# Three of four weight sums of a seven-product MLP move to GpSimd, and the order of its products is derived anew

## The chip, the cores and the metric

The kernel runs on one core of a Trainium2 chip. The metric is the device time of one execution in microseconds (us). TensorE is called PE in the profile, VectorE DVE, ScalarE ACT, GpSimd POOL and SyncE SP; SP issues most of the loads.

## The reference

A decoder trunk of two layers over 256 tokens of width 2048: an attention mixer (MLA), then a Mamba-2 mixer, each followed by a dense MLP of width 8192. The change touches the two MLPs alone:

```python
def squared_relu_mlp(h, w_in, w_out):
    u = jax.nn.relu(h @ w_in)
    return (u * u) @ w_out
```

All values are float32. `h` is 256 x 2048, `w_in` 2048 x 8192, `w_out` 8192 x 2048; every weight is read from memory once per layer, in tiles of 128 x 1024 float32 (512 KB).

## The kernel before

**Split weights.** A float32 product is made of three fp32r products: a weight tile `raw` is split into `wh` (ScalarE, a copy to fp32r, line 102) and `wl = raw - wh` (VectorE, line 103), and the left operand is split in the same way. Every unit of work is one weight tile of 128 x 1024, so each unit costs ACT one copy and DVE one subtraction of 128 x 1024, whatever it is used for. The pools hold six `raw` tiles, four `wh` and four `wl`: the conversion of a unit can begin only when the unit four places ahead of it has been multiplied.

**The MLP.** The hidden width is worked off in eight steps p = 0 to 7. Step 0's hidden block is computed in the plain way ("c" units, eight for each of two column halves of 512, twelve matmuls each). In steps 1 to 7 the block of 256 x 2048 by 2048 x 1024 is computed with seven half-size products in place of eight (Winograd's form of Strassen's scheme): M1, N7, N5, N6, N4, M2, N3, each in four units d = 0 to 3 of six matmuls ("s" units). With b11, b12, b21, b22 the four quarters of the weights for one d, the right operands are

- M1: b11; M2: b21; N3: b22
- N7: b12 + b22; N5: b12 + b11; N6: b11 + (b12 + b22); N4: b21 + (N6's operand)

so four sums of 128 x 1024 per d, sixteen per step. The left operands (sums of `h`) are made once per MLP (`combinations`). The output product of the step before ("o" units, four for each of four column blocks, twelve matmuls each) fills in between: the hidden block of step p - 1 is multiplied by `w_out` while step p's is made.

**Who makes the sums before.** `seven` (lines 171 to 212): N7, N5 and N6 are DVE additions (line 183), made at conversion time, in place. N4 is made by a DMA: once N6's operand has been split, GpSimd's queue issues a load of b21 that adds onto the tile of b11 (line 199). The tile of b11 lies in a pool of its own, `rx` (four buffers), b12 and b22 in `raw`.

**Order.** TensorE's order is written out by `plan` and `merged` (lines 1333 to 1388): they walk a list of the seven products and a list of filler units ("c" and "o"), with estimates of TensorE's and VectorE's work. The same plan makes the list of weight loads (`sequence`). On the other engines the instructions of a step stand in an order found at build time. `Flow.next` keeps, ahead of the unit that TensorE is at, six units loaded and three converted (`ahead = (6, 3)`). After the last unit of a product, its bank in PSUM is combined with others on DVE (`after`, lines 598 and 599), goes through relu and square on ACT, and is transposed by TensorE (four matmuls, line 310), with the result split once more (DVE line 300). After the fourth unit of an output block DVE adds two PSUM banks of 128 x 512 to the residual (line 419).

Of the kernel before, what the change touches and what calls it, by code (L numbers as in the profile page):

```python
# [20 lines left out]
F32 = mybir.dt.float32  # L21
# [7 lines left out]
P = 128  # L29
# [29 lines left out]
class Unit:  # L59

    def __init__(self, key, nk, n, loads, make):
        self.key, self.nk, self.n, self.loads, self.make = key, nk, n, loads, make


class Load:
# [4 lines left out]
class Flow:  # L72


    def __init__(self, nc, pools, seq, ahead):
        self.nc, self.pools, self.ahead = nc, pools, ahead
        self.units = [u for entry in seq for u in entry(self)]
        self.loaded, self.done, self.at = 0, 0, 0
        self.split = {}

    def fetch(self, ld, cuts=None, beside=None):
# [24 lines left out]
    def narrow_halves(self, raw):  # L106
# [8 lines left out]
            out.append(t)  # L115
        return out

    def convert(self, upto):
        while self.done < min(upto, len(self.units)):
            self.load(self.done + 1)  # L120
            self.split[self.done] = self.units[self.done].make()
            self.done += 1

    def next(self, key):
        j, u = self.at, self.units[self.at]
        assert u.key == key, (u.key, key)
        self.load(j + 1 + self.ahead[0])
        self.convert(j + 1 + self.ahead[1])
        self.at += 1
        return u, self.split.pop(j)  # L130
# [39 lines left out]
def seven(layer, p, src):  # L170

    state = {}

    def quarter(d, i, j):
        return src[2 * i + d // 2, 2 * p + j][:, (d % 2) * 1024:(d % 2) * 1024 + 1024]

    def unit(flow, name, d):  # L180
        nc = flow.nc
        st = state.setdefault(d, {})
        add = lambda out, a, b: nc.vector.tensor_tensor(st[out].tile, st[a].tile, st[b].tile, ALU.add)
        halves = lambda q: flow.halves(st[q].tile, 1024)

        def make():
            if name == "N7":
                add("b22", "b12", "b22")
                out = halves("b22")
                if d in LATE5:  # L190
                    nc.gpsimd.dma_start(st["b12"].tile, quarter(d, 0, 0), accum_op=ALU.add)
                return out
            if name == "N5" and d not in LATE5:
                add("b12", "b11", "b12")
                return halves("b12")
            if name == "N6":
                add("b11", "b11", "b22")
                out = halves("b11")
                nc.gpsimd.dma_start(st["b11"].tile, quarter(d, 1, 0), accum_op=ALU.add)  # L199
                return out  # L200
            return halves({"M1": "b11", "N4": "b11", "N5": "b12"}.get(name, name))

        def load(k, pool, q):
            st[k] = Load(pool, quarter(d, *q))
            return st[k]

        loads = {"M1": lambda: [load("b11", "rx", (0, 0))],
                 "N7": lambda: [load("b12", B12, (0, 1)), load("b22", "raw", (1, 1))],
                 "M2": lambda: [load("M2", "raw", (1, 0))], "N3": lambda: [load("N3", "raw", (1, 1))]}
        return Unit(("s", layer, p, name, d), 2, 512, loads.get(name, list)(), make)  # L210

    return unit


class Trunk:
# [274 lines left out]
    def mlp(self, layer, gain):  # L490
        with ExitStack() as ctx:
            mp = ctx.enter_context(self.tc.tile_pool(name="mlp", bufs=1, reuse_waits="tile"))
            for name, n in (("rx", 4), ("ry", 1)):
                self.flow.pools[name] = ctx.enter_context(self.tc.tile_pool(name=name, bufs=n, reuse_waits="tile"))
            self.flow.ahead = (4, 3)
            self.mlp_body(mp, layer, gain)

    def combinations(self, mp, xa):


        nc = self.nc
        f, S = {}, {}

        def whole(i, t):
            pool = "rx" if len(f) < 3 else "ry"
            f[i, t] = self.flow.pools[pool].tile([P, 1024], F32, tag=pool, name=self.name("xf"))
            h, lo = (v.rearrange("p k n -> p (k n)").bitcast(F32) for v in xa[i, t])
            nc.vector.tensor_tensor(f[i, t], h, lo, ALU.add)
            return f[i, t]

        def put(name, src, pool):
            S[name] = [(self.ktile(self.xtp).rearrange("p a b -> p (a b)") if pool is None else
                        pool.tile([P, 1024], F32R, name=self.name("s" + name))).rearrange("p (k n) -> p k n", n=P)
                       for _ in range(2)]
            self.split_out(*[v.rearrange("p k n -> p (k n)") for v in S[name]], src)

        def less(out, a, b):
            nc.vector.tensor_tensor(out, a, b, ALU.subtract)
            return out

        def one():
            a21, a11 = whole(0, 1), whole(0, 0)
            a22 = whole(1, 1)
            less(a22, a21, a22)
            put("N5", a22, mp)
            f["s1"] = a22

        def two():
            put("N7", less(f[0, 1], f[0, 1], f[0, 0]), mp)
            put("N6", less(f[0, 0], f[0, 0], f["s1"]), mp)  # L530
            a12 = whole(1, 0)
            less(a12, a12, f[0, 0])

        def three():
            put("N3", f[1, 0], None)

        return S, (one, two, three)

    def mlp_body(self, mp, layer, gain):
# [65 lines left out]
        def after(name, p):  # L605
            if name == "M1":
                v["m1"] = self.scratch()
                nc.scalar.activation(v["m1"], bank["M1"], AF.Copy)
            elif name in ("N5", "N6"):
                v[name] = p  # L610
                if v.get("N5") != p or v.get("N6") != p:
                    return
                w, c, e = (self.scratch() for _ in range(3))
                sub(w, bank["N6"], v["m1"])
                plus(c, bank["N5"], w)
                plus(w, bank["N7"], w)
                plus(e, bank["N7"], c)
                v["w"], v["c"] = w, c
                turn(relu_in_place(e, 1), p, 1, 1, TR[0])
            elif name == "N4":  # L620
                sub(v["w"], bank["N4"], v["w"])
                turn(relu_in_place(v["w"], 1), p, 0, 1, TR[1])
            elif name == "M2":
                plus(v["m1"], bank["M2"], v["m1"])
                turn(relu_in_place(v["m1"], 0), p, 0, 0, TR[2])
            elif name == "N3":
                plus(v["c"], bank["N3"], v["c"])
                turn(relu_in_place(v["c"], 0), p, 1, 0, TR[3])
# [693 lines left out]
             "x7", "z5", "z6", "o2a", "z7", "o2b", "o3"]  # L1322


B12 = "raw"
WARM = 9
LATE5 = ()
TR = (10, 8, 7, 7, 5)
TR_GAP = 4
PAUSE = 2.7  # L1330


def merged(p, blocks):


    main = [(n, d) for d in range(4) for n in ("M1", "N7", "N5", "N6") if n != "N5" or d not in LATE5]
    late = [(n, d) for d in range(4) for n in ("N5", "N4") if n == "N4" or d in LATE5]
    second = [(n, d) for d in range(4) for n in ("M2",)] + [("N3", d) for d in range(4)]
    units = [(b, o) for b, n in blocks for o in range(n)]
    vector = {"M1": 1.22, "N4": 1.22, "M2": 1.22, "N3": 1.22}  # L1340
    pe = 28 * 1.36 + 2.72 * len(units) + 16 * 0.11
    ve = (40 - len(LATE5)) * 1.22 + 1.22 * len(units) + 1.37 * len(blocks) + 11 * 0.68
    t = work = 0.0
    rest, done, out = -9.0, {}, []

    def ready(n, d):
        if n in ("N4", "N5"):
            return t >= done.get(("N6", d), 1e9) + 12 or (n, d) in main
        if n == "M2":
            return t >= done.get(("M1", 3), 1e9) + 7  # L1350
        if n == "N3":
            return t >= max(done.get((q, 3), 1e9) for q in ("N5", "N6")) + 7
        return True

    while main or late or second or units:
        op = next((q for q in (late, main, second) if q and ready(*q[0])), None)
        filler = t >= rest and len(units) > (4 if p == 7 and op else 0)
        if filler and (op is None or work > t * ve / pe - 2):
            b, o = units.pop(0)
            out.append(b + (o,))  # L1360
            t, work = t + 2.72, work + 1.22
            if not units or units[0][0] != b:
                rest, work = t + (PAUSE if b[0] == "o" else 10), work + 1.37
        else:
            if op is None:
                op = late or second
            n, d = op.pop(0)
            out.append(("s", p, n, d))
            t, work = t + 1.36, work + (1.22 if n == "N5" and d in LATE5 else vector.get(n, 2.44))
            done[n, d] = t  # L1370
            if n in ("N5", "N6") and d == 3 and {("N5", 3), ("N6", 3)} <= set(done):
                work += 2.73
            elif d == 3 and n in ("N4", "M2", "N3"):
                work += 0.68
    return out


# [146 lines left out]
```

## Time and profile before

| what | value |
|---|---|
| median of three runs | 2311.22 us (2311.05 to 2311.95) |
| profiled execution, its own time | 2310.92 us |
| its span, first to last instruction | 2308.7 us |
| first MLP, seven-product steps | 301.5 to 893 us of the span |
| second MLP, last seven-product unit | at about 2248 us of the span |
| loads for the MLP through SP | 256 of `mi` and 256 of `mo` into `raw`, 56 of `mi` into `rx` |
| adding loads through POOL | 56 of `mi` onto `rx` |

The profile is of one execution. A line of a group gives the source line, engine, operation, output and inputs, shape, count, then busy time, mean duration in ns, and the idle time in front. A line of waits gives who waited for whom: us in total, times, longest. A line of the timeline gives start, duration, engine, line and operation; "x2" means two of them run into one another. Durations of one DVE or PE instruction overlap with the next one's by a little, so that the distance of two starts, where the engine never idles, is what an instruction costs. In the view of one line the three numbers are shortest, median and longest duration in ns.

### The profile page before, as it was taken

Reading aid. Unit: us, or ns where it says so; the run is one execution under the profiler, and the core shown is the slowest. Engines: PE = TensorE matmul, PEld = TensorE weight load, DVE = VectorE, ACT = ScalarE, POOL = GpSimd, SP = SyncE. Lnnn points to the kernel's source line nnn. Section 1 sums busy time; section 2 is a strip of 40 time slices with the busy share of each in tenths; the row PEclk is TensorE's granted clock in tenths of the full one; section 3 lists DMA queues with packets and bytes.
Section 4 is the critical chain, followed back from the end, with each engine's and each line's share of the span. In section 5 each row is a group of like instructions: output and inputs, shape, how many; then the busy total and the mean of one; then the engine's idle time right before and its main releaser. Section 6 shows DMA issues by size and latency. Waiting matters only on the chain.

```text
span 2308.7 us, 30782 instructions
## 1 busy us (share of the span) xinstructions
PE 2302.4 (100%) x11057; PEld 1912.2 (83%) x11057; DVE 1874.8 (81%) x2318; ACT 1421.2 (62%) x1995; POOL 187.1 (8%) x227
## 2 busy tenths in 40 slices
PE   9999999999999999999999999999999999999999
PEld 8888888888888888888888888888888888888887
DVE  7776697899899897677787667656989889989895
ACT  7775465566666656565676565545566656666663
POOL 1430000000000000000122001110000000000000
PEclk9999999999999999999999999999999999999999
DMA  8444677877887877665566656656687788788874
GB/s 317 147 132 150 204 234 242 263 238 251 263 243 249 269 208 247 195 210 177 173 204 200 218 188 203 190 187 201 203 251 235 255 263 248 242 267 240 249 232 162
DMA packets 152153, 510.77 MB, mean 221 GB/s; under 512 B 17152, under 2 KB 26304, under 8 KB 152000
## 3 DMA queue, kind: packets, MB, share of 16 engines
q1 hardware_dynamic: 143712, 479.37, 63.2%
q0 software_dynamic: 8064, 29.36, 7.7%
q8 instruction: 87, 1.43, 0.3%
q14 instruction: 66, 0.54, 0.1%
q10 hardware_dynamic: 224, 0.07, 0.0%
HBM read 506.58 MB, written 2.16 MB: 220 GB/s over the span
## 4 chain that ended last, share of the span: by engine, by line
PE 96%; DVE 2%; DMA 1%; issue 0%; ACT 0%; SPq 0%; DVEq 0%
PE acc L325 13%; PE acc L326 13%; PE acc L329 13%; PE yp L595 9%; PE yp L596 9%; PE yp L594 9%; PE st L595 7%; PE st L596 7%; PE st L594 7%; PE sm L310 2%; DMA wraw<-mi 1%; DVE wl L103 1%; PE y L1240 1%; PE acc L594 1%; PE acc L596 1%; PE acc L595 1%
## 5 line engine op out<-in xcount | busy, mean ns | idle before, releaser
L102 ACT ACTIVATE wh<-wraw 128x1024 fp32r<-128x1024 f32 (+1 forms) x818 | 861.2, 1055 | 640.1 <-PE acc L326 313.5
L103 DVE TENSOR_TENSOR wl<-wraw,wh 128x1024 fp32r<-128x1024 f32 (+1 forms) x818 | 985.1, 1217 | 271.3 <-ACT wh L102 257.3
L594 PE MATMUL yp<-wh,k 128*128 128x512 f32 x896 | 349.9, 391 | 0.0
L595 PE MATMUL yp<-wl,k 128*128 128x512 f32 x896 | 349.0, 389 | 0.5 <-DVE wl L103 0.5
L596 PE MATMUL yp<-wh,k 128*128 128x512 f32 x896 | 348.8, 389 | 0.0
L325 PE MATMUL acc<-wh,xt 128*128 128x512 f32 x704 | 281.4, 400 | 0.2 <-ACT wh L102 0.2
L326 PE MATMUL acc<-wh,xt 128*128 128x512 f32 x704 | 275.1, 391 | 0.0
L102 ACT ACTIVATE wh<-wrx 128x1024 fp32r<-128x1024 f32 x168 | 178.1, 1060 | 135.7 <-PE yp L596 105.5
L103 DVE TENSOR_TENSOR wl<-wrx,wh 128x1024 fp32r<-128x1024 f32 x168 | 204.1, 1220 | 36.1 <-ACT wh L102 35.9
L595 PEld LDWEIGHTS yp<-wl,k 128*128 128x128 f32 x896 | 168.3, 188 | 35.9 <-DVE wl L103 1.4
L596 PEld LDWEIGHTS yp<-wh,k 128*128 128x128 f32 x896 | 168.2, 188 | 35.0
L325 PE MATMUL acc<-wh,k 128*128 128x512 f32 x496 | 197.0, 397 | 0.0
L594 PEld LDWEIGHTS yp<-wh,k 128*128 128x128 f32 x896 | 168.2, 188 | 34.7
L326 PE MATMUL acc<-wh,k 128*128 128x512 f32 x496 | 193.3, 390 | 0.0
L329 PE MATMUL acc<-wl,xt 128*128 128x512 f32 x704 | 188.5, 389 | 0.0
L594 PE MATMUL st<-wh,xt 128*128 128x512 f32 x448 | 176.9, 395 | 0.0
L595 PE MATMUL st<-wl,xt 128*128 128x512 f32 x448 | 174.8, 390 | 0.0
L596 PE MATMUL st<-wh,xt 128*128 128x512 f32 x448 | 174.7, 390 | 0.0
L325 PEld LDWEIGHTS acc<-wh,xt 128*128 128x128 f32 x704 | 132.6, 188 | 28.4 <-ACT wh L102 1.5
L329 PEld LDWEIGHTS acc<-wl,xt 128*128 128x128 f32 x704 | 132.2, 188 | 28.0
L326 PEld LDWEIGHTS acc<-wh,xt 128*128 128x128 f32 x704 | 132.7, 189 | 27.2 <-issue 1.0
L199 POOL DMA_DIRECT2D wrx<-mi x56 | 48.8, 871 | 1140.8 <-DVE wl L103 1035.0
(302 smaller groups left out, 3450.4 us busy)
## 6 DMA issues: line engine op xcount, KB each, us to landing
wraw<-mi SPq DMA_DIRECT2D x256, 512.0 KB, 5.1
wraw<-mo SPq DMA_DIRECT2D x256, 512.0 KB, 5.2
wraw<-si SPq DMA_DIRECT2D x160, 512.0 KB, 4.4
wraw<-so SPq DMA_DIRECT2D x64, 512.0 KB, 4.5
wrx<-mi SPq DMA_DIRECT2D x56, 512.0 KB, 5.1
wrx<-mi POOLq DMA_DIRECT2D x56, 512.0 KB, 8.2
wraw<-wo SPq DMA_DIRECT2D x32, 512.0 KB, 3.8
wraw<-ukv SPq DMA_DIRECT2D x16, 512.0 KB, 4.1
```

The lines of the kernel that those rows point to most:

```text
L102: self.last = nc.scalar.activation(h[:, v], raw[:, v], AF.Copy)
L103: nc.vector.tensor_tensor(lo[:, v], raw[:, v], h[:, v].bitcast(F32), ALU.subtract)
L199: nc.gpsimd.dma_start(st["b11"].tile, quarter(d, 1, 0), accum_op=ALU.add)
L310: self.nc.tensor.transpose(b[:, j * P:(j + 1) * P], src[:, j * P:(j + 1) * P], self.ident)
L325: nc.tensor.matmul(accs[t][:, :n], ah, wh[:, q, :], start=first and kt + q == 0, stop=False)
L326: nc.tensor.matmul(accs[t][:, :n], al, wh[:, q, :], start=False, stop=False)
L329: nc.tensor.matmul(accs[t][:, :n], lhs(kt + q, t)[0], wl[:, q, :], start=False, stop=en and q == nk - 1)
L594: nc.tensor.matmul(b, ah, wh, start=first and q == 0, stop=False)
L595: nc.tensor.matmul(b, ah, wl, start=False, stop=False)
L596: nc.tensor.matmul(b, al, wh, start=False, stop=last and q == 1)
L1240: nc.tensor.matmul(y[t][c, o], part(t)[:, c], xg[g][t][:, o], start=True, stop=True)
```

## The change

For each d the step now has four loads: b11, b12, b22 and b21 (M1, N7, N4), and later b21 and b22 once more for M2 and N3, as before. N7's sum stays with VectorE; N5, N6 and N4 are summed by GpSimd's `tensor_tensor` (twelve per step, 168 in all); no DMA adds any longer, and b21 for N4 is a plain load through SP into `raw`. b11 and b12 lie in a pool `sum` with five buffers. Sums have a counter of their own in `Flow`: they are issued two units ahead of the conversion (`SUM_AHEAD = 2`), so five ahead of TensorE. N5 and N6 no longer share an "either may come last" rule: N6 is the later one.

```diff
+    def sums(self, upto):
+        while self.added < min(upto, len(self.units)):
+            self.load(self.added + 1)
+            if self.units[self.added].add:
+                self.units[self.added].add()
+            self.added += 1
...
         self.load(j + 1 + self.ahead[0])
+        self.sums(j + 1 + self.ahead[1] + SUM_AHEAD)
         self.convert(j + 1 + self.ahead[1])
...
-            if name == "N5" and d not in LATE5:
-                add("b12", "b11", "b12")
-                return halves("b12")
-            if name == "N6":
-                add("b11", "b11", "b22")
-                out = halves("b11")
-                nc.gpsimd.dma_start(st["b11"].tile, quarter(d, 1, 0), accum_op=ALU.add)
-                return out
...
+        def add(out, a, b):
+            eng = flow.nc.vector if name in VSUM else flow.nc.gpsimd
+            return lambda: eng.tensor_tensor(st[out].tile, st[a].tile, st[b].tile, ALU.add)
...
+            "N7": (lambda: [load("b12", 0, 1), load("b22", 1, 1)], "b22", add("b22", "b12", "b22")),
+            "M1": (lambda: [load("b11", 0, 0)], "b11", None),
+            "N5": (list, "b12", add("b12", "b11", "b12")),
+            "N6": (list, "b11", add("b11", "b11", "b22")),
+            "N4": (lambda: [load("b21", 1, 0)], "b21", add("b21", "b11", "b21")),
+            "M2": (lambda: [load("M2", 1, 0)], "M2", None),
+            "N3": (lambda: [load("N3", 1, 1)], "N3", None)}[name]
...
-            for name, n in (("rx", 4), ("ry", 1)):
+            more = ctx.enter_context(self.tc.tile_pool(name="more", bufs=5, reuse_waits="tile"))
...
+SUM_AHEAD = 2
+VSUM = ("N7",)
+SUM_POOL = {"b12": "sum", "b11": "sum"}
...
+POOL_SUM = 2.6
+POOL_BACK = 2
+LAG = 2.7
...
+    main = [(n, d) for d in range(4) for n in ("M1", "N7", "N5", "N6", "N4")]
+    late = [(n, d) for n in ("M2", "N3") for d in range(4)]
...
+        op = main or (late if t >= last + LAG else None)
         filler = t >= rest and len(units) > (4 if p == 7 and op else 0)
-        if filler and (op is None or work > t * ve / pe - 2):
+        if filler and (not op or work > t * ve / pe - 4 or pool > t + POOL_BACK):
```

What `plan` makes of it in a middle step (p = 2 to 6 are alike), with the filler units as o:

```
before  M1(0) N7(0) o N5(0) N6(0) o M1(1) N7(1) o o N5(1) o N4(0) N6(1) M1(2) N7(2) o
        N5(2) N6(2) o o o N4(1) M1(3) N7(3) N4(2) N5(3) o N6(3) M2(0) o o o M2(1) M2(2)
        N4(3) o M2(3) N3(0) N3(1) N3(2) N3(3) o o
after   M1(0) N7(0) o o o N5(0) N6(0) N4(0) M1(1) N7(1) o N5(1) N6(1) o N4(1) M1(2) N7(2) o
        N5(2) N6(2) o N4(2) M1(3) N7(3) o N5(3) N6(3) o o o o N4(3) M2(0) M2(1) M2(2) M2(3)
        N3(0) N3(1) N3(2) N3(3) o o o o
```

Step 1 has 20 fillers in all, with one c after N7(0), M1(1) and N7(1) each and the next filler behind N4(2); step 7 has 20 too, with eleven of them ahead of N6(3).

In the built program DVE goes from 2249 rows to 2137, POOL from 232 to 344 (168 adds for 56 DMAs), SP has 56 loads more. In a middle step POOL's sums stand in the order N5(0) N6(0) N4(0) N5(1) N5(2) N6(1) N4(1) N6(2) N4(2) N5(3) N6(3) N4(3), and the N7 sums on DVE stand several units ahead of their conversions (N7(2)'s ahead of that of N4(0)).

More of the change, by code (lines that the diff above doesn't have):

```diff
@@ L59, with __init__ @@
 class Unit:
-    def __init__(self, key, nk, n, loads, make):
-        self.key, self.nk, self.n, self.loads, self.make = key, nk, n, loads, make
+    def __init__(self, key, nk, n, loads, make, add=None):
+        self.key, self.nk, self.n, self.loads, self.make, self.add = key, nk, n, loads, make, add
 class Load:
@@ L77, in __init__ @@
         self.units = [u for entry in seq for u in entry(self)]
-        self.loaded, self.done, self.at = 0, 0, 0
+        self.loaded, self.added, self.done, self.at = 0, 0, 0, 0
         self.split = {}
@@ L116, in narrow_halves @@
         return out
+    def sums(self, upto):
[4 more added lines that the diff above has]
+            self.added += 1
     def convert(self, upto):
         while self.done < min(upto, len(self.units)):
-            self.load(self.done + 1)
+            self.sums(self.done + 1)
             self.split[self.done] = self.units[self.done].make()
@@ L180, in unit, with load @@
     def unit(flow, name, d):
-        nc = flow.nc
         st = state.setdefault(d, {})
[L183 to L191, printed above, removed]
-                return out
-            if name == "N5" and d not in LATE5:
-                add("b12", "b11", "b12")
-                return halves("b12")
-            if name == "N6":
-                add("b11", "b11", "b22")
-                out = halves("b11")
[L199 to L204, printed above, removed]
-            return st[k]
[L207 to L210, printed above, removed]
+        def load(k, i, j):
+            st[k] = Load(SUM_POOL.get(k, "raw"), quarter(d, i, j))
+            return st[k]
+        def add(out, a, b):
+            eng = flow.nc.vector if name in VSUM else flow.nc.gpsimd
+            return lambda: eng.tensor_tensor(st[out].tile, st[a].tile, st[b].tile, ALU.add)
+        loads, of, sums = {
+            "N7": (lambda: [load("b12", 0, 1), load("b22", 1, 1)], "b22", add("b22", "b12", "b22")),
[5 more added lines that the diff above has]
+            "N3": (lambda: [load("N3", 1, 1)], "N3", None)}[name]
+        return Unit(("s", layer, p, name, d), 2, 512, loads(), lambda: flow.halves(st[of].tile, 1024), sums)
     return unit
@@ L492, in mlp @@
             mp = ctx.enter_context(self.tc.tile_pool(name="mlp", bufs=1, reuse_waits="tile"))
-            for name, n in (("rx", 4), ("ry", 1)):
-                self.flow.pools[name] = ctx.enter_context(self.tc.tile_pool(name=name, bufs=n, reuse_waits="tile"))
+            more = ctx.enter_context(self.tc.tile_pool(name="more", bufs=5, reuse_waits="tile"))
             self.flow.ahead = (4, 3)
+            self.flow.pools["sum"] = more
             self.mlp_body(mp, layer, gain)
@@ L504, in whole @@
         def whole(i, t):
-            pool = "rx" if len(f) < 3 else "ry"
-            f[i, t] = self.flow.pools[pool].tile([P, 1024], F32, tag=pool, name=self.name("xf"))
+            f[i, t] = self.flow.pools["sum"].tile([P, 1024], F32, tag="sum", name=self.name("xf"))
             h, lo = (v.rearrange("p k n -> p (k n)").bitcast(F32) for v in xa[i, t])
@@ L608, in after @@
                 nc.scalar.activation(v["m1"], bank["M1"], AF.Copy)
[L609 to L612, printed above, removed]
+            elif name == "N6":
                 w, c, e = (self.scratch() for _ in range(3))
@@ L1322 @@
              "x7", "z5", "z6", "o2a", "z7", "o2b", "o3"]
-B12 = "raw"
+SUM_AHEAD = 2
+VSUM = ("N7",)
+SUM_POOL = {"b12": "sum", "b11": "sum"}
 WARM = 9
-LATE5 = ()
 TR = (10, 8, 7, 7, 5)
@@ L1330 @@
 PAUSE = 2.7
+POOL_SUM = 2.6
+POOL_BACK = 2
+LAG = 2.7
 def merged(p, blocks):
-    main = [(n, d) for d in range(4) for n in ("M1", "N7", "N5", "N6") if n != "N5" or d not in LATE5]
-    late = [(n, d) for d in range(4) for n in ("N5", "N4") if n == "N4" or d in LATE5]
-    second = [(n, d) for d in range(4) for n in ("M2",)] + [("N3", d) for d in range(4)]
+    main = [(n, d) for d in range(4) for n in ("M1", "N7", "N5", "N6", "N4")]
+    late = [(n, d) for n in ("M2", "N3") for d in range(4)]
     units = [(b, o) for b, n in blocks for o in range(n)]
-    vector = {"M1": 1.22, "N4": 1.22, "M2": 1.22, "N3": 1.22}
     pe = 28 * 1.36 + 2.72 * len(units) + 16 * 0.11
[L1342 to L1356, printed above, removed]
+    ve = 28 * 1.22 + 1.22 * len(units) + 1.37 * len(blocks) + 11 * 0.68 + 1.22 * 4 * len(VSUM)
+    t = work = pool = 0.0
+    rest, last, out = -9.0, 0.0, []
+    while main or late or units:
+        op = main or (late if t >= last + LAG else None)
         filler = t >= rest and len(units) > (4 if p == 7 and op else 0)
-        if filler and (op is None or work > t * ve / pe - 2):
+        if filler and (not op or work > t * ve / pe - 4 or pool > t + POOL_BACK):
             b, o = units.pop(0)
@@ L1364, in merged @@
         else:
-            if op is None:
-                op = late or second
-            n, d = op.pop(0)
+            n, d = (op or late).pop(0)
             out.append(("s", p, n, d))
[L1369 to L1374, printed above, removed]
+            t, work = t + 1.36, work + (2.44 if n in VSUM else 1.22)
+            if n[1] in "4567":
+                last, pool = t, pool + POOL_SUM
+            if d == 3:
+                work += {"N6": 2.73, "N4": 0.68, "M2": 0.68, "N3": 0.68}.get(n, 0)
     return out
```

## Prediction

> **What bounds the kernel now.** I read the page's head first, then the waits of TensorE, then the windows over several steps of the first MLP.
>
> ```profile
> span 2308.7 us, 30782 instructions
> PE 2302.4 (100%) x11057; PEld 1912.2 (83%) x11057; DVE 1874.8 (81%) x2318; ACT 1421.2 (62%) x1995; POOL 187.1 (8%) x227
> ...
> PE warmed L433 <- DVE warm L430: 1.4, 1, 1.4
> PE yp L595 <- DVE wl L103: 0.5, 1, 0.5
> PE yp L910 <- DVE qn L865: 0.4, 1, 0.4
> PE acc L325 <- ACT wh L102: 0.2, 1, 0.2
> PE sm L1071 <- DVE s L1080: 0.2, 1, 0.2
> ...
> 301.50:408.00 106.50, 105.98 (x481) 87.47 (x481) 93.26 (x91) 68.39 (x75) 4.54 (x5) 1.00 0.77 234
> 408.00:492.00 84.00, 84.00 (x380) 69.58 (x379) 77.24 (x76) 53.50 (x57) 3.48 (x4) 1.00 0.82 251
> 826.00:909.00 83.00, 82.87 (x372) 67.89 (x372) 70.75 (x73) 51.78 (x57) 2.83 (x4) 1.00 0.76 232
> ```
>
> The windows give, after the stretch and its length, busy time of PE, weight load, DVE, ACT and POOL, then the granted clock (1.00). TensorE waits 2.7 us in all (the five rows), and in a middle step of an MLP it is busy 84.00 of 84.00 us while DVE is busy 77.24: TensorE sets the end, DVE is 7 us per step behind it. Is TensorE at its own rate, or only "busy"? The timeline tells:
>
> ```profile
> 479.81 0.39 PE L594 MATMUL yp<-wh,k 128*128 128x512 f32 x1
> ...
> 481.17 0.39 PE L594 MATMUL st<-wh,xt 128*128 128x512 f32 x1
> ...
> 482.53 0.60 PE L310 MATMUL sm<-cst,s 128*128 128x128 f32 x4
> 482.89 0.48 PE L594 MATMUL st<-wh,sN 128*128 128x512 f32 x1
> ```
>
> Six matmuls lie between the first two rows: 1.36 us for one seven-product unit (six matmuls), 2.72 us for a hidden or output unit (twelve). Four transposes cost 0.36 us and 0.1 more behind them. A middle step has 28 + 16 units and four groups of transposes: 28 x 1.36 + 16 x 2.72 + 4 x 0.46 = 83.4 us, and the measured steps take about 83.5. So TensorE is at its rate, and the change leaves its work as it is. What could be gained is the waits: 0.52 us of PE idle in 301.5 to 408, and in 826 to 909 a weight load 0.85 us under that of a full window, some 1 us of pace. Twice that is 3 us, 0.13%.
>
> **What the change removes, adds and moves.** Per step it takes eight adds (N5, N6) from DVE, takes four adding DMAs from POOL's queue, gives SP four plain loads in their place, and gives POOL twelve adds of 128x1024. Fourteen steps: 112 adds off DVE, 56 DMAs moved, 168 adds on POOL. The rows for these:
>
> ```profile
> L103 DVE TENSOR_TENSOR wl<-wraw,wh 128x1024 fp32r<-128x1024 f32 (+1 forms) x818 | 985.1, 1217 | 271.3 <-ACT wh L102 257.3 <-DMA wraw<-si 2.8 <-PE y L1240 1.7
> L183 DVE TENSOR_TENSOR wrx<-wrx,wraw 128x1024 f32<-128x1024 f32 x56 | 68.4, 1221 | 0.9
> L199 POOL DMA_DIRECT2D wrx<-mi x56 | 48.8, 871 | 1140.8 <-DVE wl L103 1035.0 <-issue 105.8
> ...
> 488.84 1.22 DVE L103 TENSOR_TENSOR wl<-wrx,wh 128x1024 fp32r<-128x1024 f32 x1
> 489.98 1.22 DVE L103 TENSOR_TENSOR wl<-wraw,wh 128x1024 fp32r<-128x1024 f32 x1
> ...
> 493.38 1.28 DVE L419 TENSOR_TENSOR x<-yp,x 128x512 f32<-128x512 f32 x2
> 494.58 3.49 DVE L103 TENSOR_TENSOR wl<-wraw,wh 128x1024 fp32r<-128x1024 f32 x3
> ...
> wrx<-mi SPq DMA_DIRECT2D x56, 512.0 KB, 5.1
> wrx<-mi POOLq DMA_DIRECT2D x56, 512.0 KB, 8.2
> ```
>
> A DVE operation of 128x1024 shows 1.22 us, but the next starts 1.14 us later: that is its price. One of 128x512 with an operand in PSUM costs 0.60. The eight adds save DVE 9.1 us per step, all of it beside TensorE, so they save the end nothing. A load through SP lands in 5.1 us where the adding DMA took 8.2; it is issued six units ahead (at least 6 x 1.36 = 8.2 us), so it costs nothing while SP's queue runs; if a buffer comes free late, SP's loads behind it are late too. The N7 adds stand early in DVE's queue and wait for these loads; a late one holds the subtractions behind it.
>
> The POOL adds: no add of 128x1024 on POOL is in the trace. Nearest:
>
> ```profile
> L779 POOL TENSOR_TENSOR qn<-ra,rb x8: 728/736/742, 70.8 to 164.6; 128x256 f32<-128x256 f32 x8
> L1246 POOL TENSOR_TENSOR xtm<-xtm,far x8: 1288/1293/1300, 1153.6 to 1547.8; 128x512 f32<-128x512 f32 x8
> ```
>
> From 256 to 512 elements it grows by 0.56 us; 512 more cost 1.11: 2.40 us. Upper bound twice the 512 row, 2.58; lower bound the slope alone, 2.2. I take 2.40, as the two sizes show a fixed part. Twelve are 28.8 us in a step of 83.4, so POOL alone has room. But they don't run beside DVE freely:
>
> ```profile
> 1150.97 2.55 POOL L1244 TENSOR_TENSOR xtm<-xtm,gb 128x512 f32<-128x512 f32 x2 [20.65 <-PE y L1240]
> 1205.30 2.59 POOL L1272 TENSOR_TENSOR xtm<-s,xtm 128x512 f32<-128x512 f32 x2 [17.58 <-DVE s L1262]
> 1208.91 2.09 POOL L1192 TENSOR_TENSOR s<-xtm,edge 128x512 f32<-128x512 f32 x1 [1.02 <-ACT xtm L1182]
> ...
> 1152.90 0.68 DVE L1262 SCALAR_TENSOR_TENSOR s<-s,acc 128x512 f32<-128x512 f32 x1
> 1206.66 2.31 DVE L103 TENSOR_TENSOR wl<-wraw,wh 128x1024 fp32r<-128x1024 f32 x1
> ```
>
> POOL adds from 1205.30 to 1207.89. The DVE subtraction that starts at 1206.66 takes 2.31 us in place of 1.22: it ends 1.09 after POOL's end, so it stood still until then. Behind it another subtraction runs, and POOL's operation at 1208.91 takes 2.09 where L1246's of the same size take 1.29: now POOL waited. The DVE operation at 1152.90, with one operand in PSUM, takes its 0.68 while POOL adds. So an add on POOL and a DVE operation with both inputs in SBUF exclude each other for their whole length and take turns; one with a PSUM input goes on. Every weight subtraction (L103) and N7 add is of the excluded kind.
>
> The Trainium skill, "SBUF — State Buffer", section "Who interferes with whom", has this lock as a rule: whoever starts first keeps the port pair, the other blocks fully; it speaks against this change. The trace agrees with 2.31 us against 1.22. The Trainium skill, "GPSIMD Engine Reference", section "3.1 Elementwise — side-by-side cycle accounting", gives 4497 ns for 2048 elements; half of it would be an estimate of 2.25 us, and the forecast below would fall by about 13 us.
>
> **The sum.** Per middle step the port is wanted for (44 subtractions + 4 N7 adds) x 1.14 + 12 x 2.40 = 83.5 us, as long as the step itself. Before, DVE's 56 x 1.14 left 19.6 us. That alone would nearly fit, but the twelve POOL adds all fall in the first 20 of 28 products. DVE can be only four units ahead (four wh and wl buffers). I count from when N4(0) may be converted, at the end of the second filler, to the start of N6(3):
> - TensorE: the third filler, 16 products, five fillers: 16 x 1.36 + 6 x 2.72 = 38.1 us.
> - DVE on the port: 20 subtractions and two N7 adds, 22 x 1.14 = 25.1.
> - POOL: N6(1), N4(1), N5(2), N6(2), N4(2), N5(3), N6(3), 7 x 2.40 = 16.8; the four sums ahead of these fall in the fillers before.
> - DVE with PSUM: two residual pairs, 4 x 0.60 = 2.4, half of it under POOL (no row tells; none or all is 1.2 either way): 1.2.
>
> 43.1 against 38.1: TensorE waits 5.0 us in that stretch, and the four fillers behind it let DVE catch up before the next step. The same count for the order of before, from the end of N5(0) to the start of N6(3), gives 31 x 1.14 + 3.6 = 38.9 against 44.9, no stall, as measured. First step (from the first filler's end to N4(2)): 13 x 1.14 + 5 x 2.40 = 26.8 against 12 x 1.36 + 2 x 2.72 = 21.8: 5.0. Last step, with 9 fillers in the stretch: 25 x 1.14 + 16.8 + 1.8 = 47.1 against 46.3: 0.8. Two layers: 2 x (5 x 5.0 + 5.0 + 0.8) = 61.6. The profiled execution took 2310.92 us (its span 2308.7 and 2.2 around it), the median is 2311.22; 2310.9 + 61.6 = 2372. The stall shows first at a product whose sum POOL makes: TensorE waits for wl, DVE's queue behind it (residual adds, combinations from PSUM) is late by as much, and ACT stands at the next wh because its sum is not there. The bounds (2.2 with PSUM work all hidden, 2.58 with none) give 2.4 and 7.5 us per middle step, 2343 to 2405 in all.
>
> **Rivals.** (1) Serial: DVE never finds its PSUM work or a gap while POOL adds. Then a step takes 48 x 1.14 + 19 x 0.60 + 28.8 = 94.9 us, 11.5 over TensorE's; first and last steps with four more fillers 99.5 against 94.3. 10 x 11.5 + 4 x 5.2 = 136: 2447, with 2.58 per add 2478. For it: DVE has no long gaps in the steps; against it: the tail of a step has no POOL adds, where DVE catches up. (2) Hidden: POOL takes the port only in gaps. DVE's own work falls to 66 us of 83.4, so 17 us lie idle, and 11.4 of PSUM work could cover more; 28.7 in all for 28.8 of POOL. If the sums run as far ahead as the loads, the end stays where TensorE puts it, and the 3 us of waits are all that can be had: 2308 to 2312, not slower. It decides from a lead of two more sums at the first filler (2 x 2.40 covers most of the 5.0). Against it: four buffers bound DVE's lead, and the sums write in place, so each waits for the conversion of its operand. (3) Late loads: the N7 adds wait in DVE's queue for a load whose buffer comes free late. Before, the longest such wait was 2.9 us:
>
> ```profile
> DVE wraw L183 <- DMA wraw<-mi: 21.6, 22, 2.9
> ```
>
> One of 2.9 in each middle step, on top: 2372 + 29 = 2401.
>
> **How the numbers follow.** The burst 0.55 (2372), serial 0.17 (2447), late loads 0.12 (2401), hidden 0.16 (2310). The range 2312 to 2450 leaves out part of the hidden case and the upper part of the serial one. The bound of what can be told from no change is 0.2%, 4.6 us: faster by more would need more than all waits of TensorE, 0.02; same 0.14; slower 0.84.
>
> **What would show it.** TensorE's waits for wl and wh at L594 and L595 (or their new lines) grow from under 1 us to some 60, two thirds of it at N5, N6, N4; single L103 operations of 2.3 to 3.6 us in the MLP windows; POOL adds of 2.4 us, or 3.5 when they wait their turn; steps of 88 to 89 us, with stalls ahead of N6(3) and none in the last eight products. I am wrong if PE stays at 84.00 of 84.00 in the middle steps (hidden), if L103 keeps its 1.22 us beside POOL adds (no lock), or if TensorE waits at the M2 and N3 products too (serial).

## The result and the profile after

The changed kernel takes 2510.93 us (2507.95 to 2516.78, four runs) against 2311.14 for the kernel before: a ratio of 1.0868, interval 1.0855 to 1.088. It is 200 us slower; 62 were forecast, and the time lies beyond the range. The profiled execution took 2507.95 us.

The head of its page, with busy time of each engine, and its waits of TensorE (who waited for whom: us, times, longest):

```profile
span 2506.1 us, 31047 instructions
PE 2359.4 (94%) x11057; PEld 1925.8 (77%) x11057; DVE 2042.4 (81%) x2206; ACT 1414.9 (56%) x1995; POOL 679.0 (27%) x339
...
PE yp L591 <- DVE wl L103: 67.5, 32, 4.6
PE yp L590 <- DVE x L416: 40.9, 28, 4.1
PE st L591 <- DVE wl L103: 27.7, 34, 2.4
PE acc L591 <- DVE wl L103: 3.1, 2, 1.6
PE acc L322 <- ACT wh L102: 1.8, 4, 1.2
```

With the same 11057 matmuls the span grew by 197.4 us. TensorE's idle time went from 6.3 (2308.7 - 2302.4) to 146.7 (2506.1 - 2359.4), 140.4 more, and its busy time by 57.0. Nearly all the idle time is one engine's doing, VectorE's, at two kinds of place: a `wl` that is not there (67.5 + 27.7), and a residual add (L416) that has not yet emptied the PSUM bank which the next output block wants (40.9). VectorE did less work by count, 2206 instructions in place of 2318, and was busy for longer. The groups and the view of single durations (shortest, median, longest) say with what:

```profile
L103 DVE TENSOR_TENSOR wl<-wraw,wh 128x1024 fp32r<-128x1024 f32 (+1 forms) x818 | 1147.4, 1417 | 271.3 <-ACT wh L102 265.0
L103 DVE TENSOR_TENSOR wl<-wsum,wh 128x1024 fp32r<-128x1024 f32 x168 | 302.6, 1817 | 21.7 <-ACT wh L102 20.0
L197 POOL TENSOR_TENSOR wsum<-wsum,wsum 128x1024 f32<-128x1024 f32 x56 | 187.2, 3343 | 584.5 <-DVE wraw L197 584.5
...
L103 DVE TENSOR_TENSOR wl<-wsum,wh x168: 1207/1213/3428, 308.5 to 2426.8; 128x1024 fp32r<-128x1024 f32 x168
L197 POOL TENSOR_TENSOR wsum<-wsum,wraw x56: 2394/3252/3480, 309.9 to 2418.1; 128x1024 f32<-128x1024 f32 x56
```

A weight subtraction of 1.21 us takes up to 3.43. A GpSimd add takes 2.39 us at the shortest, the 2.40 of the forecast, and 3.25 in the middle: 0.86 of it is waiting.

One step, by its timeline. First VectorE, then GpSimd, then TensorE, all of the same stretch:

```profile
512.95 3.42 DVE L103 TENSOR_TENSOR wl<-wsum,wh 128x1024 fp32r<-128x1024 f32 x1
516.30 0.68 DVE L297 TENSOR_TENSOR k<-sm,k 128x512 fp32r<-128x512 f32 x1
516.90 3.11 DVE L103 TENSOR_TENSOR wl<-wraw,wh 128x1024 fp32r<-128x1024 f32 x1
519.93 3.41 DVE L197 TENSOR_TENSOR wraw<-wsum,wraw 128x1024 f32<-128x1024 f32 x1
...
525.01 1.27 DVE L416 TENSOR_TENSOR x<-yp,x 128x512 f32<-128x512 f32 x2
...
511.98 3.31 POOL L197 TENSOR_TENSOR wsum<-wsum,wsum 128x1024 f32<-128x1024 f32 x1 [27.86 <-DVE wraw L197]
516.52 2.41 POOL L197 TENSOR_TENSOR wsum<-wsum,wraw 128x1024 f32<-128x1024 f32 x1 [1.23 <-DVE wl L103]
519.01 3.26 POOL L197 TENSOR_TENSOR wraw<-wsum,wraw 128x1024 f32<-128x1024 f32 x1
...
522.90 0.39 PE L592 MATMUL st<-wh,sN 128*128 128x512 f32 x1
525.83 0.47 PE L590 MATMUL yp<-wh,k 128*128 128x512 f32 x1 [2.54 <-DVE x L416]
...
528.19 0.63 PE L591 MATMUL yp<-wl,k 128*128 128x512 f32 x1
528.62 0.63 PE L592 MATMUL yp<-wh,k 128*128 128x512 f32 x1
```

The three sums of d = 0 each hold up an operation of VectorE. The third that is held is the sum N7(1), and the residual adds stand behind it in VectorE's queue. They begin at 525.01 and 0.8 later TensorE can begin the first filler, after 2.54 us without a matmul. Then comes a second price: matmuls start every 0.43 us, not every 0.23. The windows (PE, weight load, DVE, ACT and POOL busy, then the granted clock) show why:

```profile
523.00:619.00 96.00, 87.21 (x378) 69.75 (x376) 88.28 (x69) 52.99 (x58) 38.16 (x12) 0.98 0.65 220
526.00:531.00 5.00, 5.00 (x16) 3.93 (x16) 4.06 (x4) 0.51 (x1) 0.71 (x1) 0.66 0.64 208
```

The granted clock is 0.66 in the 5 us behind the stall, where it is 1.00 in every window quoted before the change. So a part of the 57 us of longer PE busy time is work at a slower pace, which no count of waits shows. This step lasts 96.0 us, 12.5 more than the 83.5 before.

Where in the step the 12.5 us are lost, three windows of it show: from the start of M1(0) to the end of the second filler, from there to the start of N6(3) (the stretch that the prediction counts), and the rest, up to the next M1(0). The last line is the middle stretch in the run below in which GpSimd only fills, with the same order of products:

```profile
520.40:532.98 12.58, 10.04 (x37) 7.82 (x36) 10.89 (x9) 4.25 (x4) 5.15 (x2) 0.86 0.56 167
532.98:579.13 46.15, 39.90 (x169) 31.07 (x168) 42.30 (x28) 23.50 (x23) 24.76 (x8) 1.00 0.60 200
579.13:616.38 37.25, 37.25 (x173) 30.86 (x172) 35.08 (x33) 25.23 (x30) 8.60 (x4) 1.00 0.74 261
...
501.51:539.59 38.08, 38.08 (x170) 31.53 (x168) 30.01 (x28) 23.77 (x23) 13.43 (x15) 1.00 0.75 244
```

At TensorE's rate the three are 8.16, 38.08 and 37.25 us. So 4.4 us are lost in front, 8.1 in the stretch, and none in the rest. The other middle steps are alike: the front takes 10.6 to 14.7 us, the stretch 46.1 to 51.0, and the rest 37.25 wherever another middle step follows; these steps take 95.9 to 98.9 us from M1(0) to M1(0). The ten of them lose some 143 us together, the first and the last steps the other 54 or so.

### The profile page after: what moved, and what is told of

The parts are those of the page before. It is cut to its first block, busy times and chain, and to the rows that moved or that the text cites. A ratio compares the mean times of both kernels' runs of the same rounds, so it can differ in the third digit from the quotient of the medians.

```text
span 2506.1 us, 31047 instructions
## 1 busy us (share of the span) xinstructions
PE 2359.4 (94%) x11057; PEld 1925.8 (77%) x11057; DVE 2042.4 (81%) x2206; ACT 1414.9 (56%) x1995; POOL 679.0 (27%) x339
## 4 chain that ended last, share of the span: by engine, by line
PE 63%; DVE 19%; issue 8%; DMA 7%; ACT 2%; SPq 0%; DVEq 0%; ACTq 0%
DVE wl L103 15%; PE acc L322 12%; PE acc L323 12%; PE acc L326 12%; DMA wraw<-mi 4%; PE yp L591 4%; PE yp L592 4%; PE yp L590 4%; PE st L591 3%; PE st L592 3%; PE st L590 3%; DMA wsum<-mi 2%; ACT wh L102 1%; DVE wraw L197 1%; PE sm L307 1%
## 5 line engine op out<-in xcount | busy, mean ns | idle before, releaser
L103 DVE TENSOR_TENSOR wl<-wraw,wh 128x1024 fp32r<-128x1024 f32 (+1 forms) x818 | 1147.4, 1417 | 271.3 <-ACT wh L102 265.0
L591 PE MATMUL yp<-wl,k 128*128 128x512 f32 x896 | 362.7, 405 | 51.7 <-DVE wl L103 51.7
L590 PE MATMUL yp<-wh,k 128*128 128x512 f32 x896 | 363.9, 406 | 40.9 <-DVE x L416 40.9
L592 PE MATMUL yp<-wh,k 128*128 128x512 f32 x896 | 358.9, 401 | 0.0
L197 POOL TENSOR_TENSOR wsum<-wsum,wsum 128x1024 f32<-128x1024 f32 x56 | 187.2, 3343 | 584.5 <-DVE wraw L197 584.5
L103 DVE TENSOR_TENSOR wl<-wsum,wh 128x1024 fp32r<-128x1024 f32 x168 | 302.6, 1817 | 21.7 <-ACT wh L102 20.0
L102 ACT ACTIVATE wh<-wsum 128x1024 fp32r<-128x1024 f32 x168 | 177.9, 1059 | 214.6 <-PE yp L592 120.9
L590 PEld LDWEIGHTS yp<-wh,k 128*128 128x128 f32 x896 | 173.7, 194 | 87.8 <-issue 33.9
L197 POOL TENSOR_TENSOR wsum<-wsum,wraw 128x1024 f32<-128x1024 f32 x56 | 172.4, 3078 | 210.8 <-DVE wl L103 201.3
L592 PEld LDWEIGHTS yp<-wh,k 128*128 128x128 f32 x896 | 174.4, 195 | 36.9
L197 POOL TENSOR_TENSOR wraw<-wsum,wraw 128x1024 f32<-128x1024 f32 x56 | 181.6, 3243 | 43.5 <-DMA wraw<-mi 28.7
L322 PEld LDWEIGHTS acc<-wh,xt 128*128 128x128 f32 x704 | 132.2, 188 | 30.9 <-ACT wh L102 4.2
```

Of the source, the lines that this page charges most:

```text
L102: self.last = nc.scalar.activation(h[:, v], raw[:, v], AF.Copy)
L103: nc.vector.tensor_tensor(lo[:, v], raw[:, v], h[:, v].bitcast(F32), ALU.subtract)
L197: return lambda: eng.tensor_tensor(st[out].tile, st[a].tile, st[b].tile, ALU.add)
L322: nc.tensor.matmul(accs[t][:, :n], ah, wh[:, q, :], start=first and kt + q == 0, stop=False)
L590: nc.tensor.matmul(b, ah, wh, start=first and q == 0, stop=False)
L591: nc.tensor.matmul(b, ah, wl, start=False, stop=False)
```

## The experiments

Each run's time stands beside that of the kernel before, taken with it on the same chip (medians of 2310.8 to 2311.6 us); "+" is the difference to that.

**All sums by VectorE**, the new order, loads and pools kept:

```diff
-VSUM = ("N7",)
+VSUM = ("N7", "N5", "N6", "N4")
```

(The two constants of the planner that hang on VSUM were kept as they were, so that TensorE's order is the same, instruction for instruction.)

> All four sums of a step by VectorE, none by GpSimd; order of TensorE, loads and pools as in the changed kernel. Lock theory (GpSimd adds and VectorE operations on two SBUF inputs exclude each other): VectorE has 60 x 1.14 + 11.4 = 79.8 us per step of 83.4, so 2311 to 2335 us. Rival, the new order itself (loads late for the N7 sums, residual adds late for the output banks): the 41 us that TensorE waited for residual adds stay, 2370 us or more.

Measured: 2327.43 us (ratio 1.0076, 1.0059 to 1.0093), +16. TensorE waits 0.5 us for residual adds in place of 40.9. The new order is not what costs 200 us.

**GpSimd writes but does not read**, and the others wait for it as before:

```diff
-            return lambda: eng.tensor_tensor(st[out].tile, st[a].tile, st[b].tile, ALU.add)
...
+                for _ in range(2):
+                    flow.nc.gpsimd.memset(st[out].tile, 0.01)
```

> GpSimd fills the tiles of N5, N6 and N4 twice with a constant in place of each add (the three sums are left out): it writes SBUF and reads none, ScalarE and VectorE still wait for it. Lock theory: single weight subtractions stay at 1.22 us, 2308 to 2330 us. Rival, the chain of waits through GpSimd's queue (a sum comes late to ScalarE): 2400 us or more, with subtractions of 1.22 us all the same.

Measured: 2319.99 us, +9. From three views of it: VectorE's subtractions of summed tiles, GpSimd's fills, and what VectorE's N7 sums waited for.

```profile
L103 DVE TENSOR_TENSOR wl<-wsum,wh x168: 1214/1225/1227, 304.9 to 2241.2; 128x1024 fp32r<-128x1024 f32 x168
...
L201 POOL MEMSET wsum<- 128x1024 f32 x224 | 213.8, 956 | 653.9 <-DVE wraw L197 499.9 <-DVE wl L103 100.4 <-ACT wh L102 24.4
...
DVE wraw L197 <- DMA wsum<-mi: 38.0, 12, 5.4
DVE wraw L197 <- DMA wraw<-mi: 23.1, 26, 2.4
```

Not one of the 168 subtractions is longer than 1.227 us. A chain through GpSimd of 1.9 us per sum (two fills, where an add takes 2.39), issued at the same places, costs next to nothing. And the N7 sums wait 61 us for their loads here, as long as in the changed kernel (below), with TensorE hardly late: late loads by themselves are no cause.

**The lock alone**: the same operands are read and added into a scratch tile of bfloat16, and no engine waits for the result. (Loads still wait until GpSimd has read the tile that they overwrite, 37.5 us in all in SP's queue; the N7 sums wait 43 us for loads, less than in the changed kernel.)

```diff
+            def aside():
+                for o in (slice(0, 512), slice(512, 1024)):
+                    flow.nc.gpsimd.tensor_tensor(flow.idle, st[a].tile[:, o], st[b].tile[:, o], ALU.add)
```

> GpSimd adds the same operands in two halves of 512 into a scratch tile that nobody reads (N5, N6 and N4 are multiplied without their sums): no engine waits for GpSimd's results. Lock theory: weight subtractions of up to 2.4 us beside GpSimd's halves of 1.29 us, 2400 to 2500 us. Chain rival: 2311 to 2330 us.

Measured: 2450.24 us, +139. The median subtraction of a tile that GpSimd reads too is 2.09 us:

```profile
L103 DVE TENSOR_TENSOR wl<-wsum,wh x168: 1208/2092/2325, 305.8 to 2368.5; 128x1024 fp32r<-128x1024 f32 x168
```

Two thirds of the loss come with no engine waiting for a result of GpSimd: it is GpSimd's adding beside VectorE that costs. The forecast's serial rival has 2447 with adds of 2.40 us, but 2478 with the 2.58 that two halves take.

**Holds in halves**, in the real chain:

```diff
+                for o in (slice(0, 512), slice(512, 1024)):
+                    flow.nc.gpsimd.tensor_tensor(st[out].tile[:, o], st[a].tile[:, o], st[b].tile[:, o], ALU.add)
```

> The changed kernel with each GpSimd add as two of 128x512. Theory of turns: the lock is held as long in sum (24 x 1.29 in place of 12 x 2.40 us), so 2490 to 2540 us. If what hurts beyond the lock is that a single VectorE operation stands behind 2.4 us: near the 2450 us of the run in which nobody waits for the halves.

Measured: 2480.05 us. Neither expectation: between the two. Against the lock alone (2450) it has the waits for GpSimd's results, +30; against the changed kernel (2511) shorter holds, -31, although two halves take a little longer than one add (2.58 us against 2.40).

**The old order** of products with the new sums, loads and pools (`merged` of the kernel before put in place of the new one):

> The changed kernel's sums, loads and pools with the order of products of the kernel before (N4 and fillers spread as there). If the new order has a share of its own in the loss: 2440 to 2490 us. If the GpSimd adds alone make it: 2490 to 2530 us.

Measured: 2493.91 us. The new order has a share of some 17 us; +183 remain.

**No adding DMA in the kernel before**, N4's sum by VectorE:

```diff
-                nc.gpsimd.dma_start(st["b11"].tile, quarter(d, 1, 0), accum_op=ALU.add)
+            if name == "N4":
+                add("b21", "b11", "b21")
+                return halves("b21")
```

> The kernel before with N4's sum by VectorE from a plain load, so no adding DMA and no GpSimd add: VectorE 79.8 us per step of 83.4. It tells the price of the adding DMA: 2309 to 2325 us; under 2309 it would beat both kernels.

Measured: 2328.72 us (1.0082, 1.0066 to 1.0099), +18. Four more adds of 1.14 us on VectorE cost as much in the old order as in the new one (+16): VectorE at 79.8 us of 83.4 is no longer free, and the adding DMA was worth its place. The time is a little above the range expected, and the kernel beats neither of the two.

**Spread**: all sixteen fillers of a middle step among the products whose sums GpSimd makes.

```diff
+    if 1 < p < 7:
+        fill = iter(b + (o,) for b, o in units)
...
+            for i, n in enumerate(("M1", "N7", "N5", "N6", "N4")):
+                out.append(("s", p, n, d))
+                if i != (4 if d == 0 else 0):
+                    out.append(next(fill))
```

> The changed kernel with the middle steps' sixteen fillers spread evenly behind N7, N5, N6 and N4, so that GpSimd's twelve adds fall in 28 - 8 products and all sixteen fillers (72.5 us of TensorE in place of 59.8). Burst theory (the sum of the prediction: only the bunching hurts, the step as a whole has room): the port is wanted for 74 us of 72.5, so 2320 to 2380 us. Theory of turns (each add holds up VectorE for its whole length, wherever it falls: 66 + 28.8 us of VectorE and GpSimd in turn per step of 83.4): 2440 to 2500 us.

Measured: 2441.22 us, +130, and a mean granted clock of 0.999 in place of 0.986. The spread takes 70 us of the 200 away. The time lies just inside the range of the theory of turns, but neither theory has the steps. The edit spreads the middle steps alone, and the first and last ones keep their order and their loss, which both expectations passed over. From M1(0) to M1(0) a middle step now takes 90.6 us in the mean of eight, against 83.7 without GpSimd adds (the next run): 7 lost, where the forecast's count of the port (74 us of 72.5) gives 1.5 and the theory of turns 11.5.

**The spread order without and with some GpSimd adds.** Sums by VectorE alone; N4 alone by GpSimd; N5 alone; adds at N4's place into scratch; and all twelve in halves. Each differs from the kernel above in VSUM, or in the add as shown before.

> The spread order with all four sums by VectorE, no GpSimd add: the base of the spread order. Both theories: VectorE 79.8 us per step of 83.4, 2311 to 2330 us. Above 2350 the spread order itself would have a price.

Measured: 2320.83 us, +9 (1.0018 to 1.0068).

> The spread order with only N4's sum by GpSimd, four adds per step. Theory of turns: VectorE and GpSimd in turn 75.2 + 9.6 = 84.8 us per step of 83.4, some 20 us in fourteen steps over the kernel before, 2325 to 2350 us. If every add stalls TensorE by itself, whatever room VectorE has: a third of the 130 us of twelve adds, 2350 to 2375 us.

Measured: 2388.81 us, +77. Neither: above both ranges. Four adds per step cost 68 us over the run above, and eight more only 52. I then took it that N4's sum comes too late behind N6's, now VectorE's, and tried that from two sides:

> The spread order with only N5's sum by GpSimd (four adds per step, as with N4 alone, but early: it follows on the loads and the N7 sum). If N4's sum cost so much because it comes late behind N6's sum on VectorE: 2325 to 2350 us, the price of turns. If any four adds per step cost some 68 us: 2375 to 2400 us.

> The spread order with four GpSimd adds per step at N4's place, in two halves of 512 into a scratch tile (N4's sum is left out), so that nobody waits for GpSimd. Lateness theory: 2325 to 2350 us, the price of turns alone. If each add stalls TensorE through VectorE, 2370 to 2400 us.

Measured: 2379.93 and 2408.16 us. That theory falls: an early sum (N5) costs 59 us over the spread base too. The adds into scratch cost 87, but not by the lock alone: loads wait until GpSimd has read (127.4 us in SP's queue), and the N7 sums wait 62.6 us for loads, against 5.9 in the spread base. So the two runs with real sums tell the price of four adds per step: 59 and 68 us, 4 to 5 per step, about half of the 9.6 us for which they hold the lock.

> The spread order with each GpSimd add as two of 128x512. Theory of turns: the sum of the lock is what counts where the adds are spread, so 2435 to 2450 us as with whole adds. If the length of one hold costs as it did in the bunched order (31 us): 2405 to 2420 us.

Measured: 2437.94 us, so no gain from shorter holds where they are spread; the 31 us of the halves belong to the bunched order. No loss either, though the halves take 2.2 us per step longer than the whole adds (24 x 1.29 against 12 x 2.40), some 30 us in fourteen steps, which a sum of turns would charge.

With N4 alone by GpSimd in the changed order (`VSUM = ("N7", "N5", "N6")`):

> GpSimd makes only N4's sum, four adds per step in place of twelve, VectorE the other three. Lock theory: 56 x 1.14 + 11.4 + 4 x 2.40 = 84.8 us of VectorE and lock per step of 83.4: 2315 to 2390 us, a third of the changed kernel's loss or less. If the loss comes with any GpSimd sum on the path (chain rival): 2430 us or more.

Measured: 2395.91 us, +85: above the range of the lock theory and well below the chain rival's, and again 68 over the same order without GpSimd adds.

## Why the prediction was wrong, point by point

**What bounds the kernel, and what can be gained:** right. TensorE was at its rate, every saving on VectorE lay beside it, and no run came under the kernel before.

**The lock between GpSimd and VectorE, and its price:** right, and shown. An add of 128x1024 takes 2.39 us, estimated 2.40; a subtraction beside it 3.43 us, 1.22 plus the 2.2 that it stands; with GpSimd writing only, 1.227 at most for the summed tiles.

**The step that failed: the sum.** It put the port's work of a stretch, 25.1 us of VectorE and 16.8 of GpSimd, into one bag and set it against TensorE's 38.1, with "the four sums ahead of these" done for nothing in the fillers before, and half of the PSUM work under GpSimd. It had 5.0 us per middle step and 11.6 for the four first and last steps together; 12.5 were lost in the step shown, 143 in the ten middle steps, and some 54 in the other four. What the runs show in its place:
- The sums in front are not free: 12.58 us where TensorE has 8.16 of work. They hold VectorE at 512.95, 516.90 and 519.93, and the residual adds come late behind the last hold.
- The stretch takes 46.15 us, not 43.1. VectorE does enter it with its lead: ScalarE, waiting for TensorE to free a buffer, begins N4(0)'s copy at 533.23, as the second filler ends. Then the lead is used up. VectorE is busy for 42.30 us there, and as many VectorE instructions take 30.01 where GpSimd only fills; so it stood still for some 12 us, no more than the 15.6 that the sum has (16.8, less 1.2 of PSUM work under them). But it was idle for 3.85, which the sum had at nothing, 3.0 of it in front of N7 sums whose loads were late (2.40 and 0.60), ahead of TensorE's longest wait there, at the filler behind N7(2):

```profile
533.23 1.06 ACT L102 ACTIVATE wh<-wraw 128x1024 fp32r<-128x1024 f32 x1 [1.68 <-PE yp L592]
...
535.21 1.23 DVE L197 TENSOR_TENSOR wraw<-wsum,wraw 128x1024 f32<-128x1024 f32 x1 [2.40 <-DMA wsum<-mi]
...
562.29 0.50 PE L591 MATMUL yp<-wl,k 128*128 128x512 f32 x1 [3.26 <-DVE wl L103]
```

- The other middle steps add up in the same way. Their fronts lose 2.4 to 6.5 us. In their stretches VectorE waits 2.8 to 7.6 us for late loads, and without that wait each stretch would be 42.3 to 45.1 us, close to the sum's 43.1. So of the 143 us the sum foresaw 50; some 44 were lost in front and some 44 go with the late loads. This is an account from the timeline and no test: no run has the adds in this order and the loads in time.
- The bag is no rule where the adds are spread either: it leaves 1.5 us per step, and 7 are lost. Late loads are hardly the reason there: the N7 sums wait 11.4 us for them in the whole execution. Two queues that each keep their order need not fill each other's gaps as a bag does; that is the likely reason, and not shown by itself.
- The serial rival (94.9 us per step, 2447) got 0.17 and came nearer, with 2450 for the lock alone and 2441 for the spread order. Its nearness is partly luck. Its own sign, waits of TensorE at M2 and N3, did not come: the rest of the step takes 37.25 us, TensorE's own time, so VectorE does catch up in the tail, as was held against it. Its sum for the halves of the lock alone is 2478, and in the spread steps 7 us are lost for its 11.5.
- From the lock alone (2450) to the changed kernel (2511) lie some 60 us: 30 with the waits for GpSimd's results, 31 with whole holds in place of halves, by the two differences above.

**"VectorE's queue behind it is late by as much":** named, but given no price, as if it were the same stall. It is a place of its own: 40.9 us of TensorE's waits are for residual adds, two thirds of it at the first filler behind N7(0) of the ten middle steps, where the bank of the output block before is wanted.

**What was not in the sum at all:** the clock. The stall of 2.54 us is followed by work at half pace: 0.66 in the mean of 5 us is 3.4 us at half. Over the whole execution the mean is 0.986, a loss of 35 us of clock in 2506.1. The Trainium skill, "TensorE: Matmul & The Clock Gate", section "What's actually happening", says that the array's clock falls to half after an idle window of about 3.4 us, until it has been busy again. The trace agrees on the half pace and on some 3.4 us of it, but not on the idle time: 2.54 us without a matmul were enough here. What this costs in the end no run shows by itself: the spread order in halves has a mean of 0.986 and the spread order with whole adds 0.999, and their times are 2438 and 2441 us.

**Late loads (a rival, 2401):** the waits did grow, to 57.9 us (41.4 + 16.5) from 21.6:

```profile
DVE wraw L197 <- DMA wsum<-mi: 41.4, 12, 6.0
DVE wraw L197 <- DMA wraw<-mi: 16.5, 16, 2.3
```

The run in which GpSimd only writes has 61.1 us of the same waits and loses 9 us, so by themselves they are no cause: VectorE has 8 us to spare in the stretch there (30.01 of 38.08). Beside the holds it has none, and the waits count, by the account above with 2.8 to 7.6 us in a stretch, where this rival had 2.9. So it was right in part, and got 0.12 as an alternative to the burst where the two add up. **Hidden (2310):** fell.

**What would show it:** subtractions of up to 3.4 us and adds of 2.4, or 3.3 when they wait, came as written, and so did stalls ahead of N6(3) with none in the last eight products. Steps of 88 to 89 us did not (95.9 to 98.9), nor did two thirds of the waits lie at N5, N6 and N4: the waits at `yp`, the fillers, make up 108 of 141 us.

**What stays open.** Why the first four adds per step cost as much as the next eight. The adds take VectorE's work away too (1.14 us each), and with four of them VectorE is fuller (56 port operations) than with twelve (48); that would fit, but no run varies the one without the other. It is not that a single add holds VectorE for longer there: with N4 alone in the spread order VectorE is busy for 1952.2 us, against 1928.1 with 56 adds more of its own (1.14 each), so it stood still for some 1.6 us per add, no more than in the changed kernel (1.7, below). With N4 alone GpSimd's adds become longer as well, 3.26 us in the middle and up to 8.9, which the profile doesn't explain: it may be the lock, kept by a VectorE that issues without a gap, or a wait inside the instruction.

```profile
L197 POOL TENSOR_TENSOR wraw<-wsum,wraw x56: 2389/3260/8927, 311.6 to 2304.0; 128x1024 f32<-128x1024 f32 x56
```

## What to carry to other kernels

Work given to GpSimd to relieve VectorE is no relief where both inputs of VectorE's operations lie in SBUF, GpSimd reads SBUF too, and VectorE has little room (here 7 us of 84). Each add saved VectorE 1.14 us and made it stand still for 1.7: it is busy for 2042.4 us in the changed kernel and for 1759.8 with the same 2206 instructions where GpSimd only fills, 283 us for 168 adds of 2.39. When two engines exclude each other, don't set the sum of their work against a stretch alone; look which queue stands still at which instruction, who waits for what is behind it, and what the engine was to have done before the stretch begins. A late load that cost nothing while VectorE had time to spare can cost its whole length once it has none. When the bound is TensorE at its full rate, look at the granted clock behind each stall as well as at its length.

## What the runs showed that I had not expected

- More than half the loss of twelve adds per step comes with the first four in the spread order (68 of 120 us), and over a third in the changed one (68 of 184). Four of another sum (N5 in place of N4) cost 59.
- The adding DMAs, which looked like an idle detail on a queue of their own, are worth 18 us against the same sums on VectorE (2328.72 without them).
- GpSimd fills of 128x1024 (956 ns each, 336 of them) leave VectorE's subtractions at 1.22 us: a fill does not exclude VectorE, an add that reads two tiles does. An operation with one input was not tried.
